# Dilated attention and mLSTM, one core: one more group by seven products, and three smaller moves

## The chip, the cores and the metric

The kernel runs on one core of one Trainium2 chip. The metric is the device time of one execution in microseconds. The kernel before takes 1383.32 us, the median of three runs from 1382.18 to 1385.1.

## The reference

```python
h = x                                    # 512 tokens x 1024, float32
for i in range(2):
    if i == 0:                           # dilated attention
        h = h + dilated_attention_mixer(rms_norm(h, attn_norm), positions, w_in, w_out)
    else:                                # mLSTM, 8 heads, convolution and silu on q and k
        h = h + mlstm_mixer(rms_norm(h, mlstm_norm), ...)
    g = rms_norm(h, ffn_norm[i]) @ ffn_w_in[i]
    h = h + (silu(g[..., :D_FF]) * g[..., D_FF:]) @ ffn_w_out[i]     # D_FF = 2816
return rms_norm(h, final_norm)

# the attention: 8 heads of 128, three groups of (window, dilation) = (128, 1), (512, 4), (2048, 16)
proj = (xn @ w_in).reshape(B, S, 3, 3, 8, 128)
for g, (window, dilation) in enumerate(DIL_CONFIGS):
    q, k = apply_partial_rope(proj[:, :, g, 0]) * scale, apply_partial_rope(proj[:, :, g, 1])
    o, lse = dilated_window_attention(q, k, proj[:, :, g, 2], window, dilation)
o = sum over g of softmax(lse over g) * o;  return o @ w_out
```

The rotation turns the first 32 of a head's 128 columns. All weights and results are float32.

## The kernel before

**Precision.** Every operand of a large product is split into a high half, rounded to the fast float32 format by an ACT copy, and a low half, the difference, by a DVE subtraction (`split_chunk`, L231 and L233). A product is three matmuls: high by high, high by low, low by high (SPLITS).

**Order.** The attention comes first, 0 to some 450 us: the values of all heads, then the four pairs of heads (pr), each with its three groups (g) of q and k. A group is projected in one of two ways. The plain way (`project`, L268) takes 96 matmuls of 128x512. By products (`by_products`, `qk_unit`, L1046) the 2x2 blocks of the weights (W11, W12, W21, W22) and of the tokens are combined in seven products instead of eight, in the order P1, P5, P6, P2, P7, P3, P4, each 24 matmuls of 128x256. Before, pair 0's and pair 1's first group are plain, and all others go by products. `prepare_part` subtracts blocks of weights on DVE and splits the result; `load_part` fetches the blocks on SP's queue. `Feed` prepares split weights a fixed number of steps ahead of PE.

**Attention work between the projections.** `defer(n, fn)` and `advance()` place scores, exponentials, rotations and outputs of one pair at ticks of the next pair's projection; RUN_AT lists these ticks and SCORES0_AT that of a pair's first scores. In the names, a1g0 is pair 1, group 0; `c`, `p` and `u` are the accumulators of the products; `a1s` are pair 1's scores, `a1p` their exponentials. `behind_scores`, `issue_after` and their kin keep an engine's instructions in a given order. `back` (L638, L642) returns the rotated 32 rows to q and k, by POOL copies in the first group and ACT copies in the others.

**The feed forward parts.** Both use seven products (L1658), over token operands B11, T1, T3, B22, T2, B21, T4 that `split_tokens` splits once. For B11 and T1 the low half is made by a negated copy on ACT and an accumulating DMA on POOL's queue (L1520); for the others by a DVE subtraction (L1522). `f0` and `f1` are the two layers' parts, `f0j4` a tile of output columns in the first. `f0S` are sums for the second matrix product, which POOL's queue accumulates by DMA (L1780).

**mLSTM.** Each of the eight heads has three steps: `decay` (one matmul `m1nb`, L2207, an addition and exponentials `m1e`), `scores` (`m1s`, L2227, multiplied into `m1e` by DVE), and `numerators` (`m1num`, L2239, then denominators, a root and the output row `m1yt`, L2261). HEAD_AT gives for each head three ticks, at which these steps are issued among the projections `mqk`, `mv` and `mo`. A step that shares a tick with others is issued in the order of registration, and each engine runs its instructions in the order that results.

Of the kernel before, what the change touches and what calls it, by code (L numbers as in the profile page):

```python
# [11 lines left out]
F32 = mybir.dt.float32  # L12
# [5 lines left out]
P = 128  # L18
# [16 lines left out]
C3 = float(np.float32(TWO_PI - C1 - C2))  # L35
SCORES0_AT = 7
RUN_AT = (1, (4, 4.5, 5, 7, 7, 8, 9), (14.4, 15.4), (4, 5, 4))
PRODUCTS_FROM = 2
LAST_AT = (2, (3,), (), (4, 4, 4))
STACK_AT = (9, 11, 15, 17)  # L40
HEAD_AT = ((9, 10, 12), (10, 11, 13), (12, 13, 15), (13, 14, 16), (15, 16, 18), (16, 17, 19), (18, 19, 21),
# [33 lines left out]
def tile_hybrid_dilated_attn_mlstm(  # L75
# [341 lines left out]
    with ExitStack() as actx:  # L417
# [199 lines left out]
        def rope(qk, rot, blocks, first=0, end=4, direct=False):  # L617

            at = slice(R * first, R * end)
            a, sh = rot[0][at], rot[1][at]  # L620
            nc.vector.stream_shuffle(sh, a, shift)
            nc.vector.tensor_tensor(a, a, cosn[at], op=ALU.mult)
            nc.vector.tensor_tensor(sh, sh, sinn[at], op=ALU.mult)
            two_m = lambda t: t.rearrange("p (m s) -> p m s", m=2)
            if direct:
                for q in range(first, end):
                    nc.vector.tensor_tensor(halves(qk[q // 2][:R], q % 2), two_m(rot[0][quarter(q)]),
                                            two_m(rot[1][quarter(q)]), op=ALU.add)
                return
            nc.vector.tensor_tensor(a, a, sh, op=ALU.add)  # L630

            def back(by_pool=False):
                for q in range(first, end):
                    if blocks:
                        for m in range(2):
                            to, src = turned(qk, q, m, True), packed(rot, q, m, True)
                            if by_pool:
                                nc.gpsimd.tensor_copy(to, src)  # L638
                            else:
                                nc.scalar.activation(to, src, AF.Copy)  # L640
                    else:
                        nc.scalar.activation(halves(qk[q // 2][:R], q % 2), two_m(rot[0][quarter(q)]), AF.Copy)  # L642
            return back
# [31 lines left out]
        def attention_pair(pr, qks):  # L675
# [35 lines left out]
            def scores0(q, k):  # L711

                inner = True
                for i in range(2):
                    for b2 in range(2):
                        sp = score_bank(i, "%ss0" % nm)
                        o, parts = 0, []
                        for b in (2 * b2, 2 * b2 + 1):
                            lo_ = max(b - 1, 0) * P
                            w = (b + 1) * P - lo_  # L720
                            nc.tensor.matmul(sp[:, o:o + w], q[:, i, b * P:(b + 1) * P],
                                             k[:, i, lo_:lo_ + w], start=True, stop=True)
                            parts.append((b, o, w))
                            o += w
                        for b, o, w in parts:
                            pb = max(2 * b - 1, 0)
                            nc.vector.tensor_tensor_reduce(
                                p0[i][:, pb:pb + w // P, :].rearrange("p a b -> p (a b)"),
                                sp[:, o:o + w], mask_band[:, 2 * P - w:], 1.0, -3e38,
                                op0=ALU.add, op1=ALU.max, accum_out=own[:, 0, 0, i, b:b + 1])  # L730
                    if inner:
                        behind(negate, 0, i, engine=DVE)
                        if i and pr:
                            held_exps.append(lambda i=i: exponentials(0, i, False))
                        else:
                            exponentials(0, i, False)
                        run_late(i)
                ahead_of_splits[0] = last_on(DVE)

                def exps():  # L740
                    for i in range(2):
                        exponentials(0, i)
                if inner:
                    ahead_of_casts[0] = last_on(ACT)
                else:
                    defer(1, lambda: behind(exps, engine=ACT))
# [178 lines left out]
        def load_part(pr, g, key):  # L925
            if g > 2:
                pr, g = pr + 1, 0
            if pr == HEADS // 2:
                return
            if pr == 0 and key == "W11":  # L930
                t = place(("w1", "s1")[g - 1], "a0g%dW11" % g, (P, 1024))
            else:
                pool_, tag, bufs = (ap2, "wa", 1) if key == "W11" else (wp, "wraw", W_BUFS)
                t = pool_.tile([P, 1024], F32, tag=tag, name="a%dg%d%s" % (pr, g, key), bufs=bufs)
            k0, c0 = (int(key[1]) - 1) * 4 * P, g * 3 * D + (int(key[2]) - 1) * D + pr * 256
            nc.sync.dma_start(four_k(t), w_in[k0:k0 + 4 * P, c0:c0 + 256].rearrange("(k p) n -> p k n", p=P))
            parts_of.setdefault((pr, g), {})[key] = t
# [3 lines left out]
        def prepare_part(pr, g, name):  # L941
            b = parts_of[pr, g]

            def less(out, x, y):
                with behind_scores():
                    nc.vector.tensor_tensor(b[out], b[x], b[y], op=ALU.subtract)
            src = {"P1": "W11", "P5": "W11", "P6": "W11", "P2": "W21", "P7": "W12", "P3": "W22", "P4": "W21"}[name]
            if name == "P5":
                less("W11", "W12", "W11")
            elif name == "P6":  # L950
                less("W11", "W22", "W11")
            elif name == "P7":
                with tc.issue_after(sixth[0]) if (pr, g) == (1, 2) else nullcontext():
                    less("W12", "W22", "W12")
            whl = split_chunk((b[src], 1024, four_k, "a%dg%d%s" % (pr, g, name)))
            if name == "P5" and not late[0]:
                sixth[0] = last_on(DVE)
            follows = g < 2 or by_products(pr + 1, 0)
            if name == "P2":
                less("W21", "W21", "W11")  # L960
                if follows:
                    load_part(pr, g + 1, "W11")
            elif name == "P7" and follows:
                load_part(pr, g + 1, "W12")
            elif name in ("P3", "P4") and follows:
                load_part(pr, g + 1, src)
            return whl

        def qk_unit(pr, g, qk, then=None):
# [57 lines left out]
            for n, name in enumerate(QK_ORDER):  # L1027
# [40 lines left out]
                if n == 6:  # L1068
                    with behind_scores() if g == 2 else nullcontext():
                        back = rope(qk, rot, g == 0)  # L1070
                    if g == 0:
                        defer(1, lambda: back(True))
                    elif g == 2:
                        ahead_of_splits[0] = last_on(DVE)
                        back()
                        ahead_of_casts[0] = last_on(ACT)
                    else:
                        defer(1, lambda: behind(back, engine=ACT))
# [165 lines left out]
        def prepare_values(u, name, hf):  # L1244
# [14 lines left out]
            following = {"P1": "W11", "P7": "W12", "P3": "W22", "P4": "W21"}.get(name)  # L1259
            if following is not None:  # L1260
                load_block(u + 1, following, hf)
            return whl

        def left(name, a, kk, m):
# [7 lines left out]
        def values_phase():  # L1272
# [16 lines left out]
            def finish(u, name):  # L1289
# [10 lines left out]
                elif name == "P2":  # L1300
                    t = place("st0", nm + "c11")
                    copy(t, acc["c11"])
                    stored(u, t, 0, 0)
                elif name == "P7":
                    add(out["v5"], acc["u"])
                    stored(u, out["v5"], 1, 1)
                elif name == "P3":
                    add(out["u2"], acc["p5"])
                    stored(u, out["u2"], 0, 1)
                else:  # L1310
                    t = place("st1", nm + "c21")
                    copy(t, acc["u"])
                    stored(u, t, 1, 0)

# [52 lines left out]
        vctx.close()  # L1367
        ap2 = pool(actx, "attn2")
        spare.append(ap2)
        feed.ahead = 3  # L1370
        todo = attention_pair(0, qks)
        run(todo[0])

# [9 lines left out]
        for pr in range(1, HEADS // 2):  # L1383
            qks = []
            following = attention_pair(pr, qks)
            follow(todo, RUN_AT)
            project_pair(pr, qks, lambda fn=following[0]: defer(SCORES0_AT, lambda: run(fn)))
            todo = following
        last_values, last_bring = todo[3], todo[6]
# [95 lines left out]
    def ffn_in(layer, fp, pair, rbc, hook, following, hid, during):  # L1485
# [38 lines left out]
        def normalized():  # L1524
# [28 lines left out]

            raw["T4"] = raw["B21"]
            nc.vector.tensor_tensor(raw["T4"], raw["B21"], raw["T2"], op=ALU.subtract)
            split_tokens("T4")

        steps = normalized()
        STEPS = 2
# [461 lines left out]
    with ExitStack() as mctx:  # L2021
# [263 lines left out]
        at_tick(8, exponents)  # L2285
        for p, t in enumerate(STACK_AT):
            at_tick(t, lambda p=p: stack(p))
        for n, fn in enumerate((decay, scores, numerators)):
            for hh, ts in enumerate(HEAD_AT):
                at_tick(ts[n], lambda hh=hh, fn=fn: fn(hh))  # L2290
        for hh, t in LAST_OUTPUTS.items():
            at_tick(t, lambda hh=hh: outputs(hh))
        for pr, cs in ((2, (0, 2)), (3, (1, 3))):
# [254 lines left out]
```

## Time and profile before

| | us |
|---|---|
| median of three runs | 1383.32 |
| lowest, highest | 1382.18, 1385.1 |
| profiled execution, its own time | 1381.85 |
| its span in the trace | 1380.1 |
| PE busy | 1363.8 |
| DVE busy | 1127.4 |
| ACT busy | 806.2 |
| POOL busy | 183.0 |

The span is the time from the first to the last instruction of the profiled execution; its own time has 1.75 us more around it. Busy times are sums over the span. PE's matmuls overlap one another, so a busy PE says that its queue was never empty, not that it ran at its peak.

### The profile page before, as it was taken

How to read it: one execution, taken by the hardware profiler on the slowest of the kernel's cores; microseconds unless marked ns; L12 is line 12 of the kernel's file. 1: busy time of each engine (PE TensorE's matmuls, PEld its weight loads, DVE VectorE, ACT ScalarE, POOL GpSimd, SP SyncE). 2: the span in 40 equal slices, each digit the busy share in tenths (PEclk: the TensorE clock that was granted, in tenths of full speed). 3: DMA queues.
4: the chain of work that ended last, by engine and by line, in shares of the span. 5: the costliest groups of instructions: out<-in, count | busy, mean ns of one | idle time of the engine just before them, and what ended most of it. 6: DMA issues, size and time to landing. Idle time of an engine off the chain costs nothing. (4 is left out here: it accounts for less than half of the span.)

```text
span 1380.1 us, 23153 instructions
## 1 busy us (share of the span) xinstructions
PE 1363.8 (99%) x9028; PEld 1253.3 (91%) x9028; DVE 1127.4 (82%) x1782; ACT 806.2 (58%) x1297; POOL 183.0 (13%) x264
## 2 busy tenths in 40 slices
PE   9999999999999999999999999999999999999998
PEld 7898889999998889999999998888888899999886
DVE  7988668897975598788778799899858988887887
ACT  6766566777673444444476364786534544458854
POOL 3000013030402010000010110123102230001213
PEclk9999999999999999999999999999999999999999
DMA  9354245365576356323361743324334553335963
GB/s 311 112 176 137 92 139 184 130 183 169 172 264 208 105 139 167 123 73 111 123 167 63 168 125 92 92 64 121 92 123 122 148 174 115 123 113 131 200 162 106
DMA packets 140214, 193.85 MB, mean 140 GB/s; under 512 B 8996, under 2 KB 105060, under 8 KB 140104
## 3 DMA queue, kind: packets, MB, share of 16 engines
q1 hardware_dynamic: 120128, 140.73, 32.3%
q0 software_dynamic: 18752, 51.43, 15.4%
q8 instruction: 71, 1.16, 0.4%
q10 hardware_dynamic: 1224, 0.21, 0.1%
q14 instruction: 39, 0.32, 0.1%
HBM read 167.30 MB, written 22.54 MB: 138 GB/s over the span
## 5 line engine op out<-in xcount | busy, mean ns | idle before, releaser
L1805 POOL DMA_DIRECT2D f1T<-in_ffn_w_out_dram x15 | 17.8, 1185 | 207.7 <-DMA f1P_2w_w<-in_ffn_w_out_dram 136.4
L1780 POOL DMA_DIRECT2D f0S<-in_ffn_w_out_dram x10 | 8.7, 874 | 259.3 <-DVE f0hid L1697 173.2
L2337 POOL DMA_DIRECT2D hD<-hB x32 | 21.7, 697 | 68.5 <-DVE hB L2334 68.5
L268 PE MATMUL mo<-n_h,mo_k_l 128*128 128x512 f32 x64 | 25.3, 395 | 0.0
L268 PE MATMUL mo<-n_l,mo_k_h 128*128 128x512 f32 x64 | 25.2, 393 | 0.0
L268 PE MATMUL awo<-ao_h,awo_k_h 128*128 128x512 f32 x64 | 25.2, 393 | 0.0
L268 PE MATMUL mqk<-n_h,mqk_k_h 128*128 128x512 f32 x64 | 25.2, 393 | 0.0
L268 PE MATMUL mwo<-yo_l,mwo_k_h 128*128 128x512 f32 x64 | 25.1, 393 | 0.0
L268 PE MATMUL mo<-n_h,mo_k_h 128*128 128x512 f32 x64 | 25.1, 392 | 0.0
L268 PE MATMUL awo<-ao_h,awo_k_l 128*128 128x512 f32 x64 | 25.1, 391 | 0.0
L268 PE MATMUL f1j<-n_h,f1j_h 128*128 128x512 f32 x64 | 25.0, 391 | 0.0
L268 PE MATMUL f0j<-n_h,f0j_h 128*128 128x512 f32 x64 | 25.0, 391 | 0.0
L268 PE MATMUL mqk<-n_l,mqk_k_h 128*128 128x512 f32 x64 | 25.0, 391 | 0.0
L268 PE MATMUL awo<-ao_l,awo_k_h 128*128 128x512 f32 x64 | 25.0, 391 | 0.0
L268 PE MATMUL mqk<-n_h,mqk_k_l 128*128 128x512 f32 x64 | 25.0, 391 | 0.0
L268 PE MATMUL mwo<-yo_h,mwo_k_l 128*128 128x512 f32 x64 | 25.0, 391 | 0.0
L268 PE MATMUL f0j<-n_h,f0j_l 128*128 128x512 f32 x64 | 24.9, 390 | 0.0
L268 PE MATMUL f1j<-n_h,f1j_l 128*128 128x512 f32 x64 | 24.9, 390 | 0.0
L268 PE MATMUL f0j<-n_l,f0j_h 128*128 128x512 f32 x64 | 24.9, 389 | 0.0
L268 PE MATMUL f1j<-n_l,f1j_h 128*128 128x512 f32 x64 | 24.9, 389 | 0.0
L268 PE MATMUL mwo<-yo_h,mwo_k_h 128*128 128x512 f32 x64 | 24.9, 391 | 0.0
L233 DVE TENSOR_TENSOR v1P_l<-v1W,v1P_h 128x1024 fp32r<-128x1024 f32 x14 | 17.1, 1224 | 9.2 <-ACT v1P_h L231 9.1
(2716 smaller groups left out, 6006.6 us busy)
## 6 DMA issues: line engine op xcount, KB each, us to landing
f0j_w<-in_ffn_w_in_dram SPq DMA_DIRECT2D x17, 512.0 KB, 4.1
f1j_w<-in_ffn_w_in_dram SPq DMA_DIRECT2D x17, 512.0 KB, 6.0
f1T<-in_ffn_w_out_dram POOLq DMA_DIRECT2D x15, 512.0 KB, 7.0
f0hid<-in_ffn_w_in_dram SPq DMA_DIRECT2D x9, 512.0 KB, 5.6
f1hid<-in_ffn_w_in_dram SPq DMA_DIRECT2D x9, 512.0 KB, 5.3
v0W<-in_attn_w_in_dram SPq DMA_DIRECT2D x8, 512.0 KB, 6.8
v1W<-in_attn_w_in_dram SPq DMA_DIRECT2D x8, 512.0 KB, 3.7
awo_k_w<-in_attn_w_out_dram SPq DMA_DIRECT2D x8, 512.0 KB, 4.7
```

The costliest lines, as they stand in the source:

```text
L233: nc.vector.tensor_tensor(lo[:, :n], raw[:, :n], hi[:, :n].bitcast(F32), op=ALU.subtract)
L268: nc.tensor.matmul(acc, whl[a][:, k, m * P:(m + 1) * P], pairs[b][kk], start=(kk == 0 and (a, b) == SPLITS[0]), stop=(kk == nk - 1 and (a, ...
L1780: nc.gpsimd.dma_start(t, src[1][:, ks], accum_op=ALU.add)
L1805: nc.gpsimd.dma_start(view(to), weight_rows(hk * UNITS + u, n), accum_op=ALU.add)
L2337: nc.gpsimd.dma_start(hD[k // 4].rearrange("(b i) x -> i b x", i=R)[:, :, c0:c0 + R], t[R * a_:R * (a_ + 1)])
```

## The change

```diff
-PRODUCTS_FROM = 2
+PRODUCTS_FROM = 1
+FIRST_AT = (2,) + RUN_AT[1:]
...
             def back(by_pool=False):
                 for q in range(first, end):
-                    if blocks:
+                    if by_pool and not blocks and q > 1:
+                        nc.gpsimd.tensor_copy(halves(qk[q // 2][:R], q % 2), two_m(rot[0][quarter(q)]))
+                    elif blocks:
...
+                            if i:
+                                feed.fill(3)
                             exponentials(0, i, False)
...
-            if pr == 0 and key == "W11":
+            if (pr, g, key) == (1, 0, "W11"):
+                t = ap.tile([P, 1024], F32, tag="rot", name="a1g0W11")
+            elif pr == 0 and key == "W11":
...
-            follows = g < 2 or by_products(pr + 1, 0)
+            follows = g < 2 or (pr and by_products(pr + 1, 0))
...
                     elif g == 2:
                         ahead_of_splits[0] = last_on(DVE)
-                        back()
+                        back(True)
...
+            if u == len(UNITS) - 1 and hf == 1:
+                for key in {"P2": ("W11",), "P6": ("W12", "W22"), "P3": ("W21",)}.get(name, ()):
+                    load_part(1, 0, key)
...
-                    t = place("st1", nm + "c21")
+                    t = (ap.tile([P, 2, SEQ], F32, tag="vu", name=nm + "c21") if u == len(UNITS) - 1 else
+                         place("st1", nm + "c21"))
...
-        feed.ahead = 3
...
-            follow(todo, RUN_AT)
+            follow(todo, RUN_AT if pr > 1 else FIRST_AT)
...
             nc.vector.tensor_tensor(raw["T4"], raw["B21"], raw["T2"], op=ALU.subtract)
-            split_tokens("T4")
+            split_tokens("T4", True)
...
-        for n, fn in enumerate((decay, scores, numerators)):
-            for hh, ts in enumerate(HEAD_AT):
-                at_tick(ts[n], lambda hh=hh, fn=fn: fn(hh))
+        for hh in (4, 0, 1, 2, 3, 5, 6, 7):
+            for t, fn in zip(HEAD_AT[hh], (decay, scores, numerators)):
+                at_tick(t, lambda hh=hh, fn=fn: fn(hh))
```

Pair 1's first group goes by seven products. Its block W11 lies in the place of the rotation's tile, its four blocks are loaded while the last values are computed, and the last value result (c21) is copied into another tile than the score tile of pair 0 inherits. Pair 0's scores of the second and third group come one tick later. In the third group of pairs 1 to 3 the rotated rows return to k by POOL and to q by ACT, as before. T4's low half in both feed forward parts is made as that of B11 and T1. The mLSTM steps are registered head by head, head 4 first.

DVE at pair 1's first group, before: the low halves of q's weights (`a1g0q_k_l`, two of them) stand between the last values (`v1u`) and the score reductions of pair 0 (ISA, `a0p`).

```order
L1284 TENSOR_TENSOR v1u_1579<-v1p_1470,v1u_1579 128x512
L1284 TENSOR_TENSOR v1u_1579<-v1p_1471,v1u_1579 128x512
L233 TENSOR_TENSOR a1g0q_k_l<-a1g0q_k_w,a1g0q_k_h 128x1024 x2
L727 ISA a0p_1702,a0own<-a0s_1704,acst 128x128
L727 ISA a0own 128x1
L727 ISA a0p_1702,a0own<-a0s_1704,acst 128x256
```

DVE at the same place now; `a1g0P_l` is the low half of a product's weights and `a1g0W` a block that another is subtracted from.

```order
L1294 TENSOR_TENSOR v1u_1585<-v1p_1470,v1u_1585 128x512
L1294 TENSOR_TENSOR v1u_1585<-v1p_1471,v1u_1585 128x512
L234 TENSOR_TENSOR a1g0P_l<-a1g0W_1492,a1g0P_h 128x1024
L953 TENSOR_TENSOR a1g0W_1492<-a1g0W_1531,a1g0W_1492 128x1024
L234 TENSOR_TENSOR a1g0P_l<-a1g0W_1492,a1g0P_h 128x1024
L953 TENSOR_TENSOR a1g0W_1492<-a1g0W_1533,a1g0W_1492 128x1024
L730 ISA a0p_1707,a0own<-a0s_1709,acst 128x128
```

Two low halves have become two low halves and two subtractions; the others follow the reductions.

ACT in the first feed forward part, before, around the high half of T4; `f0j4v` and `f0j4u` are copies of accumulators, `f0j4S_h` and `f0j4A_h` high halves of weights.

```order
L1670 ACTIVATE f0j_u<-f0j_c_5291 128x512
L1517 ACTIVATE f0T4h<-f0x_5061 128x1024
L231 ACTIVATE f0j4S_h<-f0j_w_5263 128x1024
L1675 ACTIVATE f0j4v_5353<-f0j_p_5328 128x512
L231 ACTIVATE f0j4S_h<-f0j4A_5266 128x1024
L1680 ACTIVATE f0j4u_5383<-f0j_u 128x512
```

ACT at the same place now:

```order
L1680 ACTIVATE f0j_u<-f0j_c_5384 128x512
L1527 ACTIVATE f0T4h<-f0x_5154 128x1024
L1529 ACTIVATE f0T4l<-f0T4h 128x1024
L1685 ACTIVATE f0j4v_5447<-f0j_p_5422 128x512
L232 ACTIVATE f0j4S_h<-f0j_w_5356 128x1024
L232 ACTIVATE f0j4S_h<-f0j4A_5359 128x1024
L1690 ACTIVATE f0j4u_5477<-f0j_u 128x512
```

The negated copy `f0T4l` stands ahead of two casts and `f0j4u`. POOL's queue now, where the DMA that completes it goes out:

```order
L1530 DMA f0T1l<-f0t_5305 128x1024
L1790 DMA f0S_3_7528<-in_ffn_w_out_dram 128x512
L1790 DMA f0S_1_7412<-in_ffn_w_out_dram 128x512
L1790 DMA f0S_3_7529<-in_ffn_w_out_dram 128x512
L1530 DMA f0T4l<-f0x_5154 128x4x256
```

Three accumulations of `f0S` stand ahead of it.

PE in the mLSTM, before, at the first scores of head 0 and the decay row of head 1:

```order
L2227 MATMUL m0s<-qs_0_9186,ks_0_9185 128x512
L2207 MATMUL m1nb<-mneg,sel 128x512
L2228 MATMUL m0s<-ql_0_9191,ks_0_9185 128x512
L2227 MATMUL m0s<-qs_0_9186,ks_0_9185 128x384
L2228 MATMUL m0s<-ql_0_9191,ks_0_9185 128x384
```

PE at the same place now:

```order
L2237 MATMUL m0s<-qs_0_9280,ks_0_9279 128x512
L2238 MATMUL m0s<-ql_0_9285,ks_0_9279 128x512
L2237 MATMUL m0s<-qs_0_9280,ks_0_9279 128x384
L2238 MATMUL m0s<-ql_0_9285,ks_0_9279 128x384
L2217 MATMUL m1nb<-mneg,sel 128x512
```

Three matmuls of the scores have moved ahead of the decay row. Likewise the numerators of head 1 (`m1num`), which stood among the value projections `mv`, now follow the first half of the next projection `mqk`:

```order
L269 MATMUL mqk_0_9592<-n_h_8737,mqk_k_h 128x512
L269 MATMUL mqk_0_9592<-n_l_8738,mqk_k_h 128x512
L269 MATMUL mqk_0_9592<-n_h_8737,mqk_k_l 128x512
L2249 MATMUL m1num<-vaug,m1e 128x129 x10
L269 MATMUL mqk_1_9593<-n_h_8735,mqk_k_h 128x512
```

They are reached some 30 matmuls after the numerators of head 0 sooner than before.

## The prediction

> **What bounds the kernel now.** I read the head of the page first.
>
> ```profile
> span 1380.1 us, 23153 instructions
> PE 1363.8 (99%) x9028; PEld 1253.3 (91%) x9028; DVE 1127.4 (82%) x1782; ACT 806.2 (58%) x1297; POOL 183.0 (13%) x264
> PEclk9999999999999999999999999999999999999999
> ```
>
> PE is busy for 1363.8 of 1380.1 us and its granted clock is level in all forty slices, so the end moves only through what PE has to do or through its remaining waits. Those are in the view of waits, filtered to PE.
>
> ```profile
> PE m1num L2239 <- DVE m0yt L2261: 1.2, 1, 1.2
> PE m1nb L2207 <- ACT m0e L2217: 1.0, 1, 1.0
> PE f0j_u L1658 <- ACT f0j4u L1680: 0.9, 1, 0.9
> PE f1j_u L1658 <- ACT f1j4u L1680: 0.8, 1, 0.8
> PE a1s L781 <- ACT a1g_k L642: 0.8, 1, 0.8
> ...
> PE a2g1u L1046 <- DVE a2g_k L1016: 0.4, 1, 0.4
> PE a3g1u L1046 <- DVE a3g_k L1016: 0.4, 1, 0.4
> ```
>
> Every wait is short and happens once. The first five, which the edits aim at, add up to 4.7 us. That bounds what the three scheduling edits can return; only the seven products take matmul time away.
>
> The profiled execution took 1381.85 us, 1.75 us outside its span of 1380.1. It lies 1.5 us below the median of the three runs (1383.32) and just below their lowest (1382.18). I make the sum on the trace and take its difference from the median. About 0.2%, or 2.8 us, is what a measurement of this kernel can tell from no change.
>
> **Pair 1's first group.** From the chain of waits and the timeline of PE:
>
> ```profile
> 947.35 5.45 PE mo L268 x24
> 1104.85 2.88 PE f1j_c L1658 x24
> ...
> 176.78 0.58 PE L268 MATMUL a1g0q<-xa_h,a1g0q_k_h 128*128 128x512 f32 x1
> ...
> 202.63 0.28 PE L1046 MATMUL a1g1c<-xa_h,a1g1P_h 128*128 128x256 f32 x1
> ```
>
> A plain 128x512 matmul follows the one before after 5.45 / 24 = 0.227 us, a 128x256 one of the products after 2.88 / 24 = 0.120. The group now takes 96 of the first kind, 21.8 us; afterwards seven products of 24 of the second, 7 x 2.88 = 20.2 us. PE saves 1.6 us, if everything arrives. What other engines pay is seen by stage, in the table of windows (after the span: PE, PEld, DVE, ACT, POOL).
>
> ```profile
> 170.00:176.78 6.78, 6.78 (x36) 5.79 (x34) 2.23 (x2) 2.26 (x3) 1.21 (x2) 1.00 0.74 240
> 176.78:202.63 25.85, 25.85 (x132) 21.98 (x131) 17.54 (x52) 15.98 (x43) 3.69 (x6) 1.00 0.47 142
> 202.63:220.00 17.37, 17.37 (x147) 17.36 (x146) 17.37 (x32) 12.91 (x24) 7.83 (x12) 1.00 0.34 100
> ```
>
> The products add three low halves and four weight subtractions on DVE, seven operations at about 1.2 us (the 128x1024 subtraction in the rows below), 8.4 us; four 128x512 copies become four additions of half that size, which gives back about 1 us. So DVE gets about 7 us more. It has 4.5 us free from 170.00 to 176.78 and 8.3 free until 202.63, 12.8 in all: the cover is there, but from 202.63 to 220.00 there is none (17.37 of 17.37). What is left over then is paid by PE. A second block of free time comes from the tile of the last value result:
>
> ```profile
> 179.01 0.29 DVE L727 CUSTOM_DVE_ANT_0 a0p<-a0s,acst 128x128 f32<-128x128 f32 x1 [5.29 <-DMA vD_g1m<-v1c]
> ```
>
> DVE waits 5.29 us for the store of that result, whose place the score tile inherits. With c21 in another place this wait goes, so the score reductions run earlier; next late is PE itself, which they follow. ACT gets three casts and three bank copies, about 5 us, in 9.9 us of free time. The block loads go out during the values, and SP's queue is otherwise in the old order. Scores of pair 0's second and third group come one tick later; nothing waits for them but exponentials.
>
> The products two and three groups on find DVE full, and there pairs 2 and 3, which already start by products, lose 0.4 us each at their `g1u`. I charge pair 1 one such wait, near 0.6 us, and take **-1.0 us**. Bounds: -1.6 (nothing spills) and +5.4 (all 7 us of DVE spill, less 1.6).
>
> **The rope's k copies on POOL.** These are the rows at pair 1's third group, and below them the same kind of copy as POOL already does it.
>
> ```profile
> 251.33 2.36 DVE L946 TENSOR_TENSOR a2g0W<-a2g0W,a2g0W 128x1024 f32<-128x1024 f32 x2
> 251.51 1.27 ACT L642 ACTIVATE a1g_q<-rot 32x512 f32<-32x512 f32 x2 [1.92 <-DVE rot L630]
> 252.79 1.28 ACT L642 ACTIVATE a1g_k<-rot 32x512 f32<-32x512 f32 x2
> 253.48 2.72 PE L781 MATMUL a1s<-a1g_k,a1g_q 128*128 128x128 f32 x22 [0.83 <-ACT a1g_k L642]
> ...
> L638 POOL COPY a1g_q<-rot x4: 392/392/1227, 211.8 to 213.7; 32x256 f32<-32x256 f32 x4
> ...
> L638 POOL COPY a1g_k<-rot x4: 392/844/1388, 214.2 to 216.2; 32x256 f32<-32x256 f32 x4
> ```
>
> ACT does q, then k; PE resumes at 253.48, when the first k half is there (252.79 + 0.64). If POOL starts k at 251.5 beside ACT's q, and needed only twice its 0.39 us for a tile twice as wide, k would be done by 253.1 and 0.8 us of the wait would go. But POOL's copy also took 1.23 and 1.39 us:
>
> ```profile
> 211.53 1.22 DVE L233 TENSOR_TENSOR a1g1P_l<-a1g1W,a1g1P_h 128x1024 fp32r<-128x1024 f32 x1
> 212.66 2.18 DVE L868 STREAM_TRANSPOSE a0pB<-a0p 128x1920 f32<-128x1920 f32 x1
> ...
> 217.26 1.42 DVE L233 TENSOR_TENSOR a1g2P_l<-a1g2W,a1g2P_h 128x1024 fp32r<-128x1024 f32 x1
> ```
>
> The copy at 211.78 ended at 213.0, 0.25 us after DVE's subtraction; those under the transpose took 0.39; and the subtraction beside POOL's last copy took 1.42 instead of 1.22. At the new place DVE runs exactly two such subtractions (2.36 us). The first half would then end near 252.5 + 0.5 = 253.0, the second near 253.7 + 0.6 = 254.3, against 253.4 and 254.07 on ACT: 0.4 gained, 0.3 lost. I take **0**, from -0.8 to +1.3 (two copies that each wait out a subtraction and hold up the next, 255.4).
>
> [...]
>
> **T4's low half by ACT and an accumulating DMA.**
>
> ```profile
> 533.57 1.22 DVE L1522 TENSOR_TENSOR f0T4l<-f0x,f0T4h 128x1024 fp32r<-128x1024 f32 x1
> 534.70 1.22 DVE L1629 TENSOR_TENSOR f0j4A<-f0j4A,f0j4S 128x1024 f32<-128x1024 f32 x1
> 536.04 1.06 ACT L231 ACTIVATE f0j4S_h<-f0j4A 128x1024 fp32r<-128x1024 f32 x1 [1.60 <-DVE f0j4A L1629]
> 537.63 0.39 PE L1658 MATMUL f0j_u<-f0T3h,f0j4S_h 128*128 128x256 f32 x1 [0.95 <-ACT f0j4u L1680]
> ...
> 533.95 0.86 POOL L1780 DMA_DIRECT2D f0S<-in_ffn_w_out_dram  x1 [0.28 <-DVE f0j4A_l L233]
> DMA to landing us min/median/max: 4.4/5.5/7.1
> ...
> 543.60 0.28 PE L1658 MATMUL f0j_u<-f0T4l,f0j4A_h 128*128 128x256 f32 x1
> ...
> DMA to landing us min/median/max: 8.3/8.3/8.3
> ```
>
> The subtraction leaves DVE, so `f0j4A` is done 1.1 us earlier; but ACT's new negation stands ahead of its two casts and `f0j4u`, so ACT is the next late one, and P7 starts about 0.5 us earlier, at 537.1. The last product reads T4l, then at 543.1. Its DMA can go out at 534.9, behind three accumulations of `f0S`. The one like it, `f0T1l`, took 8.3 us (the last line); the three before it, 4.4 to 7.1 (the line above). 534.9 + 8.3 = 543.2, and near 544.0 with the queue ahead: PE waits about 1 us. The first FFN: **+0.5 us**, from -0.6 (5.3 us, landing in time) to +5.7 (the DMA begins when the last `f0S` has landed, 541.0 + 8.3 = 549.3, that is 6.2 late, less 0.5). In the second FFN its POOL queue holds one gain broadcast rather than three accumulations, and its `f1T1l` landed in 5.3:
>
> ```profile
> DMA to landing us min/median/max: 5.3/5.3/5.3
> ```
>
> There I take **-0.3** of the 0.8, bounds -0.8 and +2.
>
> **mLSTM by head.**
>
> ```profile
> 880.00:1000.00 120.00, 116.80 (x656) 99.56 (x656) 103.00 (x290) 77.91 (x205) 26.61 (x36) 1.00 0.35 93
> 882.60 0.39 PE L2228 MATMUL m0s<-ql,ks 128*128 128x512 f32 x1
> ...
> 914.20 1.11 DVE L2261 TENSOR_SCALAR m0yt<-m0num,m0rr 128x128 f32<-128x128 f32 x4
> ...
> 878.38 1.28 ACT L2214 ACT_TABLE_LOAD   x1
> ```
>
> PE idles 3.2 us in 880 to 1000, which bounds the gain. Three score matmuls now run ahead of `m1nb`, about 0.6 us from 882.60 on, and take that much off its wait. `m1num` moves from 913.5 to about 908 (36 matmuls of 0.227 and the scores after `m0num` at 898); `m0yt`, which frees its banks, moves ahead of the next convolution. Following its new order with these durations it begins near 906.8 instead of 914.20. It comes just in time, and about 1.1 of the 1.2 us goes. ACT's order gains two table loads of 1.28 us, which I charge with 0.2. Sum **-1.5**, from -3.2 to +5 (`m0yt` no earlier, the fourth rival).
>
> **The sum.** -1.0 + 0 + 0.5 - 0.3 - 1.5 = -2.3 us: 1383.3 - 2.3 = **1381.0 us**.
>
> **Rivals.**
>
> 1. *All waits go.* For it: each is single and short. -1.6 - 0.8 - 0.6 - 0.8 - 3.2 = -7.0 at most; near -5.5 is likely, 1377.8 us. Against it: waits were only moved before, too (`a2g1u`, `a3g1u`).
> 2. *DVE is the bound in the attention.* For it: 17.37 of 17.37 after 202.63, and POOL's copies hold DVE. Pair 1 gains nothing (+1.0) and the copies cost in pairs 1 and 2 (+1.0): -0.3, 1383.0 us. [...]
> 3. *T4l lands late.* For it: three accumulations ahead of it, 8.3 us for `f0T1l`. At 8.3 us after 539.5, half way to the last `f0S`, it lands at 547.8, 4.7 late: +4.2 instead of +0.5, 1384.7; with the bound of 549.3, 1386.2.
> 4. *Slower: the numerator waits.* `m1num` now stands on PE where it is reached near 908, while `m0yt` still ends a chain over ACT, which has two more table loads on it, and over a dozen small DVE steps between which the score products of the next head stand. If the chain ends no earlier than it does now, `m1num` waits about 914 - 908 = 6 us instead of 1.2, and all later work of PE queues behind it: 1383.3 - 0.8 (the other parts) - 0.4 (`m1nb` less the loads) + 4.8 = 1386.9. It makes the kernel slower by more than 2.8 us once this wait exceeds 5.2 us. Against it: DVE has 17 us free of 120 there, and its order puts `m0yt` ahead of the convolution it followed.
>
> The change does what it says, by its order; a rival that it doesn't is left out.
>
> **How the numbers follow.** Forecast 0.38, with its own range 1379.3 to 1382.5 (pair 1 at -1.6 and T4l in time, or pair 1 at 0 and `m1num` half gained); of it 0.16 lies past the 2.8 us and 0.22 within. Rival 1: 0.22, faster. Rival 2: 0.12, 0.08 within and 0.04 slower. Rival 3: 0.14, 0.05 within and 0.09 slower, as little else has to miss. Rival 4: 0.14, slower. So faster 0.38, same 0.35, slower 0.27. The range takes in each rival alone and leaves out the far end of the first, and two that cost time together: 1377.0 to 1387.5.
>
> **What would show it.** In the new trace pair 1's first group should hold only products, its `a1g1c` starting about 1 us earlier; the wait of `a0p` on `vD_g1m` should be gone, with a short wait at pair 1's `g1u` or `g2u`. POOL's k copies should take over 1 us each beside DVE's subtractions. `f0j_u` should wait under 0.5 us at P7 and about 1 us at T4l. `m1nb` and `m1num` should wait under 0.5 us. A wait on T4l over 3 us, DVE waits over 2 us in pair 1, or `m1num` waiting over 2 us would make the forecast wrong.

## The result, and the profile after

The changed kernel takes 1377.77 us (median of 7 runs, 1377.52 to 1378.48), the kernel before 1382.83 beside it (7 runs): a ratio of 0.9967, 95% interval 0.9957 to 0.9976, 5.1 us less. A later comparison of the same two (last experiment) gave 0.9972 [0.9962, 0.9983], 3.5 us. The profiled execution took 1378.38 us against 1381.85, also 3.5 us, so the traces hold that much to be explained; the other 1.6 us of the first comparison is the place of the two profiled executions among their runs (before's 1.0 under its median, after's 0.6 over).

The head of the page after, and PE's waits:

```profile
span 1376.6 us, 23337 instructions
PE 1362.3 (99%) x9100; PEld 1254.8 (91%) x9100; DVE 1131.3 (82%) x1787; ACT 812.7 (59%) x1303; POOL 196.8 (14%) x272
PEclk9999999999999999999999999999999999999999
```

```profile
PE a1g1u L1053 <- DVE a1g_k L1023: 1.1, 1, 1.1
PE m4s L2237 <- DVE m4e L2239: 1.0, 1, 1.0
PE f1j_u L1668 <- ACT f1j4u L1690: 0.6, 1, 0.6
...
PE m1nb L2217 <- ACT m0e L2227: 0.4, 1, 0.4
```

Three of the five waits aimed at are gone (`f0j_u`, `a1s`, `m1num`), `m1nb` and `f1j_u` are smaller, and two new ones of 1.0 us have come: pair 1's `a1g1u` and head 4's `m4s`. The list does not say where 3.5 us went; a ledger by stage does. Each number is the time from the start of the first matmul of one tile to that of another on PE's timeline:

| from, to | before | after | difference | products alone |
|---|---|---|---|---|
| pair 1's first group (`a1g0`, `a1g1`) | 25.86 | 24.15 | -1.71 | 24.14 |
| its second and third (`a1g1`, `a2g0c`) | 43.21 | 45.26 | +2.05 | 45.27 |
| pair 1's last scores (`a2g0c`, `a2g0u`) | 10.33 | 9.19 | -1.14 | 10.04 |
| end of the attention (`awo`, `f0j`) | 51.23 | 50.89 | -0.34 | 50.69 |
| first feed forward's products (`f0j_c`, `fo`) | 182.63 | 181.43 | -1.20 | 181.54 |
| mLSTM (`mqk`, `mwo`) | 147.79 | 146.20 | -1.59 | 147.77 |
| second feed forward's products (`f1j_c`, `finc`) | 182.53 | 182.86 | +0.33 | 182.48 |

All other stretches together make +0.14. The last column is experiment 2 below. The -0.34 at the end of the attention is not traced to a cause; profiles of one kernel differ there by 0.2.

**Pair 1.** Its rows on PE's timeline after, and on DVE's below them:

```profile
176.64 0.47 PE L1053 MATMUL a1g0c<-xa_h,a1g0P_h 128*128 128x256 f32 x1
...
200.79 0.36 PE L1053 MATMUL a1g1c<-xa_h,a1g1P_h 128*128 128x256 f32 x1
...
219.55 0.39 PE L1053 MATMUL a1g1u<-xa_h,a1g1P_h 128*128 128x256 f32 x1 [1.06 <-DVE a1g_k L1023]
...
213.16 2.41 DVE L860 TENSOR_SCALAR a0p<-a0p,a0cf 128x128 f32<-128x128 f32 x8
215.61 2.18 DVE L873 STREAM_TRANSPOSE a0pB<-a0p 128x1920 f32<-128x1920 f32 x1
218.81 0.68 DVE L1023 TENSOR_TENSOR a1g_k<-a1g1u,a1g1vu 128x512 f32<-128x512 f32 x1
```

The same three on DVE before:

```profile
208.89 2.13 DVE L855 TENSOR_SCALAR a0p<-a0p,a0cf 128x128 f32<-128x128 f32 x8
212.66 2.18 DVE L868 STREAM_TRANSPOSE a0pB<-a0p 128x1920 f32<-128x1920 f32 x1
218.60 0.68 DVE L1016 TENSOR_TENSOR a1g_k<-a1g1u,a1g1vu 128x512 f32<-128x512 f32 x1
```

PE reaches pair 1's second group 1.84 us earlier (200.79, not 202.63), but DVE's factors and transpose of pair 0 come 4.3 and 3.0 us later, and the addition that frees the bank of `a1g1u` comes no earlier than before (218.81, not 218.60). Three low halves of the second group's weights that followed the factors before now stand ahead of them. DVE was full there already:

```profile
200.00:210.00 10.00, 10.00 (x75) 9.48 (x74) 9.93 (x26) 7.25 (x14) 0.00 (x0) 1.00 0.11 31
210.00:220.00 10.00, 10.00 (x86) 10.00 (x85) 10.00 (x12) 7.00 (x13) 7.83 (x12) 1.00 0.48 143
```

```profile
200.00:210.00 10.00, 10.00 (x86) 10.00 (x86) 9.96 (x19) 6.69 (x11) 5.31 (x5) 1.00 0.01 2
210.00:220.00 10.00, 8.94 (x74) 8.73 (x74) 9.93 (x18) 6.84 (x14) 5.72 (x8) 1.00 0.77 228
```

These are the windows before (first fence) and after; the fourth number is DVE: 9.93 and 10.00 of 10 before, 9.96 and 9.93 after, while PE falls to 8.94. DVE's free time lies earlier, in the first group:

```profile
183.60 1.23 DVE L234 TENSOR_TENSOR a1g0P_l<-a1g0W,a1g0P_h 128x1024 fp32r<-128x1024 f32 x1 [2.89 <-ACT a1g0P_h L232]
...
189.60 0.42 DVE L790 CUSTOM_DVE_ANT_0 a0p<-a0s,acst 128x256 f32<-128x256 f32 x1 [0.90 <-PE a0s L786]
```

It waits 2.89 us for a cast that ACT does only at 182.54, behind pair 0's exponentials, and 0.90 us for score matmuls. After 189.60 its next wait of more than 0.12 us ends at 221.84. So 29 us of work without a break stand ahead of the addition at 218.81.

**The k copies.** Pair 1's third group after, in order of time:

```profile
249.59 2.76 DVE L953 TENSOR_TENSOR a2g0W<-a2g0W,a2g0W 128x1024 f32<-128x1024 f32 x2
249.84 2.99 POOL L636 COPY a1g_k<-rot 32x512 f32<-32x512 f32 x2 [5.13 <-DVE rot L631]
251.44 1.27 ACT L645 ACTIVATE a1g_q<-rot 32x512 f32<-32x512 f32 x2
...
251.75 3.73 PE L786 MATMUL a1s<-a1g_k,a1g_q 128*128 128x128 f32 x32
```

The rotation is ready at 249.8, ACT comes to its q copies only at 251.44, and POOL has used the time between: PE runs its 32 score matmuls without a stop.

**The first feed forward.** DVE's longest wait there, before and after:

```profile
521.93 1.23 DVE L1629 TENSOR_TENSOR f0j4S<-f0j_w,f0j4A 128x1024 f32<-128x1024 f32 x1 [3.04 <-DMA f0T1l<-f0t]
```

```profile
519.59 1.22 DVE L1639 TENSOR_TENSOR f0j4S<-f0j_w,f0j4A 128x1024 f32<-128x1024 f32 x1 [2.04 <-DMA f0T1l<-f0t]
...
L1530 POOL DMA_DIRECT2D f0T1l<-f0t x1: 896/896/896, 512.3 to 512.3; - x1
...
DMA to landing us min/median/max: 7.3/7.3/7.3
```

`f0j4S` takes the place of raw T1 and so waits until T1's own accumulating DMA has landed: 7.3 us after its issue instead of 8.3. This is T1's DMA, which the change does not touch, and not T4's. T4's landed in time:

```profile
L1668 PE MATMUL f0j_u<-f0T4l,f0j4A_h x8: 283/283/284, 541.1 to 543.6; 128*128 128x256 f32 x8
...
L1530 POOL DMA_DIRECT2D f0T4l<-f0x x1: 1651/1651/1651, 532.1 to 532.1; - x1
...
DMA to landing us min/median/max: 7.6/7.6/7.6
```

532.1 + 7.6 = 539.7, and PE reads it at 541.1.

**mLSTM.** The numerator's rows after:

```profile
904.40 1.13 DVE L2271 TENSOR_SCALAR m0yt<-m0num,m0rr 128x128 f32<-128x128 f32 x4
...
905.20 1.05 PE L2249 MATMUL m1num<-vaug,m1e 128*128 128x129 f32 x8
```

It starts without a wait. A new wait has come at head 4:

```profile
926.82 0.87 ACT L2227 ACTIVATE m4e<-m4nb,bcol 128x128 f32<-128x128 f32 x3
...
925.93 2.36 DVE L234 TENSOR_TENSOR mo_k_l<-mo_k_w,mo_k_h 128x1024 fp32r<-128x1024 f32 x2
...
928.89 1.14 DVE L2239 SCALAR_TENSOR_TENSOR m4e<-m4s,m4e 128x512 f32<-128x512 f32 x2
...
929.62 0.39 PE L2237 MATMUL m4s<-qs,ks 128*128 128x256 f32 x1 [0.96 <-DVE m4e L2239]
```

The third block of scores takes the bank of the first, which is free once DVE has multiplied the first into `m4e`. ACT has the exponentials for that ready by 927.69. DVE comes to it only at 928.89, since two low halves of `mo`'s weights and the small steps of head 2's denominators stand ahead of it, with no wait over 0.04 us between them. So DVE's order makes this wait, not ACT's table loads, of which there are now eight instead of six.

### The profile page after: what moved, and what is told of

The parts are those of the page before. It is cut to its first block, busy times and chain, and to the rows that moved or that the text cites. A ratio compares the mean times of both kernels' runs of the same rounds, so it can differ in the third digit from the quotient of the medians.

```text
span 1376.6 us, 23337 instructions
## 1 busy us (share of the span) xinstructions
PE 1362.3 (99%) x9100; PEld 1254.8 (91%) x9100; DVE 1131.3 (82%) x1787; ACT 812.7 (59%) x1303; POOL 196.8 (14%) x272
```

## The experiments

Diffs are against the changed kernel unless another is named; ratios are to the kernel before, run on the same chip. Stage times are those of the ledger.

**1. Without the products.**

```diff
-PRODUCTS_FROM = 1
+PRODUCTS_FROM = 2
...
-            follow(todo, RUN_AT if pr > 1 else FIRST_AT)
+            follow(todo, RUN_AT)
```

With it go the loads, the place of c21 and the ticks that belong to the products; these are not separated from the products by any run.

> The changed kernel with pair 1's first group plain again (with its loads, tile places and ticks as before); the other three edits stay. Theory from the changed trace (the seven products reach the end of pair 1 no earlier, because DVE holds them up at a1g1u and a1g2u by 1.2 and 0.4 us, and lost nothing either): within 0.5 us of the changed kernel's 1377.8. Rival, the prediction's term: 1.0 us slower than it, 1378.8, with pair 1's third group ending 1.0 us later. If all 1.6 us had been kept: 1379.4.

1379.92 us, 0.9987 [0.9978, 0.9996], more than each of the three forecasts; its trace is 1.9 us longer than the changed kernel's (1378.5 against 1376.6). The two stretches return to 25.86 and 43.11 us, so the products gain 1.71 and lose 2.15 there. But two other stages change, which the prediction had not tied to them: the last scores take 10.87 instead of 9.19 us, the first feed forward 182.61 instead of 181.43. The first is seen at the k copies:

```profile
251.22 2.76 DVE L951 TENSOR_TENSOR a2g0W<-a2g0W,a2g0W 128x1024 f32<-128x1024 f32 x2
251.40 1.29 ACT L645 ACTIVATE a1g_q<-rot 32x512 f32<-32x512 f32 x2 [1.97 <-DVE rot L631]
251.46 3.00 POOL L636 COPY a1g_k<-rot 32x512 f32<-32x512 f32 x2 [10.12 <-DVE rot L631]
...
252.96 3.28 PE L784 MATMUL a1s<-a1g_k,a1g_q 128*128 128x128 f32 x27 [1.37 <-POOL a1g_k L636]
```

The same two copies take the same 3.0 us, but here the rotation comes 1.6 us later, so POOL and ACT start together and PE waits 1.37 us for POOL. The second is T1's DMA: landing after 8.8 us, DVE waiting 3.5 us.

```profile
DVE f0j4S L1637 <- DMA f0T1l<-f0t: 3.5, 1, 3.5
```

**2. The products alone** (the kernel before with that edit only).

> The kernel before with only the edit to pair 1's first group (products, loads, tile places, ticks); k by ACT, T4 by DVE and the mLSTM order as before. Theory by stages: the group itself 1.7 us shorter, its two successors 2.05 longer (DVE behind them), the wait at a1s 0.3 shorter, and the first feed forward part about 1 us shorter although nothing in it is edited: together -1.0 to -1.5 us against the kernel before. Rival, the prediction's term: -1.0, all of it ahead of pair 2, and the feed forward part at its old 182.6 us. Rival, the medians of the run without the products: -2.1.

1380.59 us, 0.9989 [0.998, 0.9998]; its trace is 1.1 us shorter than before, and the theory by stages holds. Pair 1's three stretches take 79.45 us, before 79.40: in the attention the edit is worth nothing. The first feed forward takes 181.54 us, though nothing in it is edited, with T1's DMA landing in 7.2 us; in the other kernels with the products that use this DMA it takes 7.3 or 7.4.

**3. The k copies back on ACT.**

```diff
-                        back(True)
+                        back()
```

> The changed kernel with the rotated k rows of the third groups returned by ACT again. Theory: the POOL copies took away the whole wait at a1s, so without them the wait of about 0.8 us before a1g_k is back in pair 1 and the kernel is 1.0 to 1.2 us slower, 1378.9. Rival, the prediction's term of 0 (POOL's copies wait out DVE's subtractions): 1377.8, no wait at a1s.

1378.11 us, 0.9974 [0.9965, 0.9983]. The last scores take 10.04 instead of 9.19 us, and the old wait of `a1s` on ACT's `a1g_k` is back, at 0.6 us. The medians do not tell it from the changed kernel; the stage does.

So POOL's copies gain 0.85 us beside the products. Without them they lost 0.54 (10.87 against 10.33), and 0.73 in experiment 5 (11.06).

**4. T4 by DVE again.**

```diff
-            split_tokens("T4", True)
+            split_tokens("T4")
```

> The changed kernel with T4's low half subtracted by DVE again in both feed forward parts. Theory from the changed trace: the first part gained 1.2 us and the second lost 0.3, so 0.9 us slower, 1378.7, with the wait of 0.9 at f0j_u back and the one at f1j_u near 0.8. Rival, the prediction's terms (+0.5 and -0.3): 0.2 us faster, 1377.6.

1378.58 us, 0.9977 [0.9968, 0.9986]. The first feed forward takes 181.65 us: T4's edit is worth 0.2 of the 1.20 us. The wait of 0.9 us at `f0j_u` that the theory expected back does not come, here or in experiment 2.

**5. T1 by DVE in the first feed forward, without the products** (against experiment 1).

```diff
-            split_tokens("T1", True)
+            split_tokens("T1", layer > 0)
```

> The run without the products, with T1's low half in the first feed forward part subtracted by DVE instead of ACT and the accumulating DMA. Theory (the first part's 182.6 us come from DVE's wait of 3.5 us for that DMA, ahead of the sums that P7 needs): the wait goes for 1.2 us of work, and the first part takes 181.4 to 181.7 us instead of 182.6; everything else as in that run, so 1.0 us faster than it. Rival (the first part's time comes from T4's edit or from another order of the weights): it stays at 182.6.

1379.03 us, 0.9979 [0.9971, 0.9988]. With no DMA to wait for, this stage falls from 182.61 to 181.43 us, the same as with the products. That shows the mechanism: 1.2 us hung on the landing of `f0T1l`. Why it lands in 7.2 to 7.4 us with the products and in 8.3 and 8.8 without stays open: in the kernel before, the changed one and experiments 1 and 2 it is issued 11.41 us ahead of the stage's first product, with the same four DMAs beside it at the same distances.

**6. T1 by DVE in both.**

```diff
-            split_tokens("T1", True)
+            split_tokens("T1")
```

> The changed kernel with T1's low half subtracted by DVE in both feed forward parts. Theory (DVE idles some 3 us in each part ahead of the sums that P7 waits for): first part unchanged at 181.4 us, as it has no wait left; second part 182.9 to 181.6 if its idle time is the wait for T1's DMA, unchanged or 1 us longer if it is another (it landed at 1073.4, DVE went on at 1076.6), since DVE then has 1.2 us more to do.

1377.5 us, 0.9964 [0.9951, 0.9978]: not to be told from the changed kernel, though its second feed forward is the shortest (181.84 us). With experiment 12 giving 182.28 and 182.86 for one kernel, and 182.01 in experiment 1 with the DMA, the gain is not shown.

**7. mLSTM by step, as before.**

```diff
-        for hh in (4, 0, 1, 2, 3, 5, 6, 7):
-            for t, fn in zip(HEAD_AT[hh], (decay, scores, numerators)):
-                at_tick(t, lambda hh=hh, fn=fn: fn(hh))
+        for n, fn in enumerate((decay, scores, numerators)):
+            for hh, ts in enumerate(HEAD_AT):
+                at_tick(ts[n], lambda hh=hh, fn=fn: fn(hh))
```

> The changed kernel with the mLSTM steps registered step by step again, not head by head. Theory: 1.7 us slower (1379.5), the waits at m1nb and m1num back at 1.0 and 1.2 us and the one at m4s gone. Rival: the waits come back but other ones go, under 0.5 us slower (1378.2).

1378.78 us, 0.9979 [0.997, 0.9987]. The stage takes 147.51 us, 1.31 more and not the 1.7 of the theory, and both old waits are back while `m4s` is gone:

```profile
PE m1num L2249 <- DVE m0yt L2271: 1.2, 1, 1.2
...
PE m1nb L2217 <- ACT m0e L2227: 1.0, 1, 1.0
```

**8. Heads in turn, 0 to 7.**

```diff
-        for hh in (4, 0, 1, 2, 3, 5, 6, 7):
+        for hh in range(8):
```

> The changed kernel with the mLSTM heads registered 0 to 7 instead of head 4 first. Theory (head 4's decay row, put ahead of head 2's numerators, brings the wait of 1.0 us at m4s, since its exponentials queue on ACT behind the table load): m4nb moves behind m2num, the wait at m4s stays or moves, mqk to mwo within 0.5 us of 146.2. Rival: head 4's place is what shortened the mLSTM, and it takes 147.2 us or more.

1378.26 us, 0.9974 [0.9965, 0.9983]. The stage takes 146.32 us and `m4s` still waits 1.0: head 4's place is worth at most the 0.1 us by which two profiles of the changed kernel differ (146.20, 146.12), and the order by head is the rest. Nor is the new wait due to head 4 being first.

**9. Pair 0's transposes behind both k additions.**

```diff
-FIRST_AT = (2,) + RUN_AT[1:]
+FIRST_AT = (2, (4, 4.5, 7, 8, 8, 9, 10)) + RUN_AT[2:]
...
-            ... lambda: transposes(0), ...
+            ... lambda: (transposes(0) if pr else behind(transposes, 0, engine=DVE)), ...
```

> The changed kernel with the transposes of pair 0's first head held on DVE until after the k additions of pair 1's second group (they stood just ahead of the addition for which a1g1u waits). Theory (DVE's order, not its whole load, makes PE wait there): the wait of 1.1 us at a1g1u goes, 0.5 to 1.2 us faster than the changed kernel's 182.83-to-1377.77 step would put it, ratio to the kernel before 0.9960. Rival (DVE's load is the bound): the wait comes back at a1g2u or later, same time, ratio 0.9967.

1380.42 us, 0.9989 [0.998, 0.9998], 2.2 us slower than the changed kernel in the second and third group (47.41). The wait of `a1g1u` went; DVE then came late with the rotation and the third group's weights, and ACT's casts, one of which PE waits for, stand behind them:

```profile
234.68 0.44 PE L1053 MATMUL a1g2p<-S4h,a1g2P_h 128*128 128x256 f32 x1 [1.90 <-ACT a1g2P_h L232]
```

The windows behind it (last but two: PE's granted clock) show a second price:

```profile
234.00:236.00 2.00, 1.32 (x6) 1.20 (x7) 2.00 (x2) 2.00 (x5) 0.00 (x0) 0.72 0.63 257
236.00:238.00 2.00, 2.00 (x11) 2.00 (x11) 1.03 (x2) 1.01 (x2) 0.00 (x0) 0.50 0.95 330
238.00:240.00 2.00, 2.00 (x18) 2.00 (x18) 2.00 (x2) 0.00 (x0) 0.00 (x0) 0.93 0.88 245
```

0.56 + 1.00 + 0.14 = 1.7 us more are lost to the clock. The move itself trades a wait of 1.06 us for one of 1.90; most of the 2.2 us is the clock.

**10. Pair 0's first head weighted by ACT.**

```diff
-                    if i and pr < HEADS // 2 - 1:
+                    if (i or pr == 0) and pr < HEADS // 2 - 1:
```

> The changed kernel with the eight factors of pair 0's first head (2.4 us on DVE, just ahead of the transposes and the k addition that a1g1u waits for) applied by ACT, as those of its second head are. Theory (DVE's load from 200 to 240 us is the bound of pair 1's second and third group): the stretch from a1g1 to a2g0 takes 43.5 to 44.3 us instead of 45.3, and the kernel is 1.0 to 1.8 us faster than the changed one, ratio to the kernel before near 0.9957. Rival (ACT, which the transposes then wait for, is the bound as much): 45.3 us or more, ratio 0.9967 or above.

1377.77 us, 0.997 [0.996, 0.9981]. DVE loses its 2.4 us of factors, but the transpose comes only 0.5 us earlier, since it now waits for ACT:

```profile
215.06 2.18 DVE L873 STREAM_TRANSPOSE a0pB<-a0p 128x1920 f32<-128x1920 f32 x1 [2.13 <-ACT a0p L858]
...
PE a1g1u L1053 <- DVE a1g_k L1023: 0.8, 1, 0.8
```

The wait is 0.8 instead of 1.1, and the two groups take 45.42 us, no less, as the rival said.

**11. Pair 0's exchange one tick earlier, and T1 by DVE.**

```diff
-FIRST_AT = (2,) + RUN_AT[1:]
+FIRST_AT = (2, (3, 3.5, 5, 7, 7, 8, 9)) + RUN_AT[2:]
...
-            split_tokens("T1", True)
+            split_tokens("T1")
```

> The changed kernel with the joint exchange of pair 0's factors a tick earlier (ticks 3 instead of 4, the transposes of pair 0 before the next product's steps) and T1 and T4 low halves subtracted by VectorE in both FFNs. Theory, the pair's chain of factors, transposes and k additions on VectorE is late because the exchange comes late in the product: one tick is one product, 2.9 us, so a1g_k's addition comes up to 2.9 us sooner, the wait of a1g1u (1.1 us) goes and the stretch from a1g1 to a2g0c falls from 45.3 us to 43.5 to 44.3; with some 1 us of the second FFN (181.8 instead of 182.9) that makes a ratio to the kernel before of 0.995. Rival, VectorE's load in these 20 us is the bound whatever the order: the stretch stays at 45.3 us or grows, only the FFN's part is left, ratio 0.9964.

Its T4 is that of the changed kernel, by ACT and DMA; only T1 goes by DVE. 1379.42 us, 0.9981 [0.9973, 0.999]. The addition comes 1.4 us earlier and `a1g1u` waits no more, but what DVE puts off for it is late instead:

```profile
217.39 0.68 DVE L1023 TENSOR_TENSOR a1g_k<-a1g1u,a1g1vu 128x512 f32<-128x512 f32 x1
...
PE a1g2u L1053 <- ACT a1g2vu L1005: 1.2, 1, 1.2
PE a1g1p L1053 <- DVE a1g1P_l L234: 1.0, 1, 1.0
...
PE a1g2u L1053 <- DVE a1g2P_l L234: 0.5, 1, 0.5
```

The two groups take 47.22 us. This fits the rival: DVE is loaded almost without a break, and a new order chooses which product waits. It is not the whole proof, since the longest of the new waits is on ACT, and experiment 10, which took 2.4 us off DVE, made ACT the late one.

**12. The changed kernel again.**

> The changed kernel once more, unaltered, on this chip. All theories: ratio 0.9967 within 0.001, the first FFN's products again 181.4 us. It tells what of the second FFN's length (182.86 us in its first profile, 181.8 to 183.0 in its variants) differs from profile to profile of one kernel, and whether f0T1l again lands in 7.2 to 7.4 us.

1378.47 us (8 runs) against 1381.95 (18 runs), 0.9972 [0.9962, 0.9983]. Every stage up to the second feed forward repeats within 0.4 us, T1's landing (7.3 us) too; the second feed forward takes 182.28 instead of 182.86 us. So 0.6 us there is a difference between profiles of one kernel.

## Why the prediction was right or wrong

The sum said -2.3 us, 1381.0; the result, 1377.77, is 3.2 us lower and lies near the low end of the range, where the first rival stood (1377.8). Of these 3.2 us, 0.5 is the base (1382.83, not 1383.32), 1.6 the place of the two profiled executions, and 1.2 lies in the traces. The direction held, but the sum came from other places than forecast: pair 1 came out 1.3 us worse than its term, the k copies 0.85 and the first feed forward 1.7 us better, for reasons that were not forecast. That they balanced so nearly is luck. The first rival's reason, that all waits go, did not hold: two came anew.

- **Pair 1's first group, -1.0.** The matmuls' saving was right: 1.71 us against 1.6. So was "a short wait at `g1u` or `g2u`", but its size failed: I charged 0.6 us and the two groups lost 2.05, so the second rival (DVE bounds the attention) described this part. The step that failed let 12.8 us of free DVE time ahead of 202.63 cover 7 us of new work by its sum, and did not ask where it lies. DVE is busy 19.8 of 24.15 us in the group, but of the 4.4 us left 4.1 lie ahead of 189.60, where it waits for ACT's cast and for scores; from there on it is full, and the work that could not be done earlier stands ahead of the addition. The prediction's own sign of being wrong, DVE waits over 2 us in pair 1, was there: 2.89 us at 183.60. Experiments 9 to 11 moved or relieved DVE's chain in three ways and none shortened the two groups.
- **The k copies, 0.** The price was right, some 1.5 us for a copy beside a subtraction, and DVE's two subtractions took 2.76 instead of 2.36 us. The groups by form show the price with and without that company:

```profile
L636 POOL COPY a1g_k<-rot x2: 1441/1468/1496, 249.8 to 251.3; 32x512 f32<-32x512 f32 x2
...
L636 POOL COPY a3g_k<-rot x2: 602/604/607, 400.0 to 400.7; 32x512 f32<-32x512 f32 x2
```

  In pair 3 DVE has no subtraction beside them, only short score reductions, and a copy takes 0.60 us. Beside the subtractions it takes 1.44 to 1.50 us; what makes the difference is not shown. The second rival's +1.0, for copies that cost time in pairs 1 and 2, was an estimate, and no run shows it: DVE's two subtractions took 0.40 us longer in pair 1 (2.76, not 2.36) and 0.42 in pair 2 (2.77, not 2.35), but PE's last scores took 1.14 us less in pair 1 and 9.24 us in pair 2, before and after. The gain of 0.85 us came from elsewhere: I set the start at 251.5, beside ACT's q, from the trace before. With the products POOL's copies start at 249.84, without them at 251.46; the lead begins at a cast of the next pair's weights by ACT, which DVE waits for 1.78 us after and 3.58 before (4.00 in experiment 1):

```profile
241.83 1.23 DVE L233 TENSOR_TENSOR a2g0P_l<-a2g0W,a2g0P_h 128x1024 fp32r<-128x1024 f32 x1 [3.58 <-ACT a2g0P_h L231]
```

```profile
239.94 1.23 DVE L234 TENSOR_TENSOR a2g0P_l<-a2g0W,a2g0P_h 128x1024 fp32r<-128x1024 f32 x1 [1.78 <-ACT a2g0P_h L232]
```

  So POOL ran ahead of ACT. Why the cast comes earlier is not followed further. The two edits were costed one by one, and this term was their meeting.
- **T4, first feed forward, +0.5.** Measured -1.20, of which T4's edit is 0.2. The wait at T4l (1 us) did not come: the landing took 7.6, not 8.3 us, and the issue stood 9.0 us ahead of its use, not 8.2. The rest is T1's landing. Its 8.3 us stood in the prediction as a price for T4's; that DVE waited 3.04 us for it, ahead of the casts that `f0j4u` and P7 follow, had no term in the sum. The third rival fell.
- **Second feed forward, -0.3.** Measured +0.33 with 0.6 us between two profiles of one kernel: not decided.
- **mLSTM, -1.5.** Measured -1.59, and 1.31 when undone. `m0yt` was placed at 906.8; this stage begins 2.5 us earlier, which makes 904.3, and it began at 904.40. The mechanism held for `m1num` (1.25 us gone) and `m1nb` (0.59 of 0.96). The term for ACT's table loads, 0.2, did not: no wait of PE is traced to them, but the new order cost 0.96 us at `m4s`, behind DVE. Smaller waits, of `m2num`, `m3num`, `m5num`, `m6num` and `m6yT`, fell from 0.99 to 0.46 together and made up half of it, so that the stage came out as forecast is in part luck. The fourth rival fell.

## What to carry to other kernels

Free time summed over a stage covers new work only where that work can already be done: look for the engine's last wait, and count what stands between it and the instruction that the next engine waits for. Where two edits meet at one buffer, cost the pair: the copies on POOL lost 0.54 us without the products and gained 0.85 beside them. And read what waits for every DMA whose landing is quoted as a price; the largest single unforecast gain here was a wait that the trace before already showed.

## What the runs showed of the hardware

In experiment 9 PE waited 1.90 us, until 234.68, and the granted clock was then 0.72 of full over 234 to 236 us, 0.50 over 236 to 238 and 0.93 over 238 to 240. The 1.7 us lost, at 0.50, make some 3.4 us below full, an estimate from these three windows. In that stretch a matmul of 128x256 followed the one before after 0.21 us instead of 0.12. Waits of 1.06 us (the changed kernel), 1.25 (the kernel before) and 1.37 (experiment 1) left the clock at 1.00 in the windows around them. The fall was seen once, and no run tested what sets it off or what ends it.
